# A two-layer hybrid decoder on one core: the low part of q over all 128 rows, and low parts of weights by a copy and an accumulating DMA

## The chip, the core and the metric

The kernel runs on one core of a Trainium2 chip. The metric is device time in microseconds, the median of the runs shown. The trace that is read here is of one further, profiled execution of the same program.

## What is computed

Two layers over 512 tokens of width 1024. Each layer normalizes x, projects it into ten parts of 512 columns, runs four mixers on them (a diagonal state space "S5", differential attention, a gated linear recurrence after a short convolution "LRU", attention into 256 memory tokens), gates each result and projects back:

```python
for layer in range(DEPTH):                       # 2
    h = rms_norm(x, norm_g[layer])
    a_u, a_g, qd, kd, vd, b_g, c_x, c_g, m_q, m_g = jnp.split(h @ w_in[layer], 10, axis=-1)
    y_a = s5_mixer(a_u, ...)
    q, k = rope_partial(qd...), rope_partial(kd...)
    o_b = diff_attention(q, k, v, lam)           # per head: softmax(q1 k1) - lam softmax(q2 k2), times v
    y_b = rms_norm(o_b, da_subln_g[layer]) * (1 - lam_init)
    y_c = rglru_mixer(c_x, ...)
    y_m = memory_attention(m_q, rms_norm(mem, ...), w_mem_kv[layer])
    mixed = concat(y_a * silu(a_g), y_b * silu(b_g), y_c * silu(c_g), y_m * silu(m_g))
    x = x + mixed @ w_out[layer]
return rms_norm(x, final_norm_g)
```

All in float32. Attention B has 4 heads of two 64-wide query and key halves each, and is causal.

## The kernel before

**Products in three passes.** A float32 product is made of operands of the type float32r. Each operand is split into a high part (a cast) and a low part (the operand less its high part), and a product is high x high + high x low + low x high. So every weight needs both parts in SBUF.

**The stream of weights.** All weights are cut into 136 pieces of 128 x 1024 elements (512 KB), 68 to a layer, in the order of `ORDER`. In layer 0 that is q, v, k, the memory's k and v, cx, au, cg, bg, mq, ag, mg, gl and four products with `w_out`; in layer 1 the products from au on come as au, mq, bg, mg, ag, cg, gl. `w_load` (L148) issues a piece's load on SP's queue into one of two `raw` buffers. `w_split` (L159) makes `whi` by a cast on ScalarE (ACT, L166) and `wlo` by a subtraction on VectorE (DVE, L172), in three buffers each, and then lets the next load go. `w_use(i)` (L176) is called where a product takes its piece i; it asks for the splits up to piece i + 2, so a piece's parts are made while the two pieces ahead of it are multiplied. A buffer of `whi` or `wlo` comes free when PE is done with the piece three back.

**Products.** `cm_block` (L495; matmuls at L508) takes the weight as the stationary operand: a unit of two pieces, 24 matmuls to a piece, in steps of twelve. The products cg, bg, mq, ag and mg are all of this kind, two units each, so twenty pieces in a row per layer. `tm_block` (matmuls at L528) takes the activations as the stationary operand, and the products with S5's output (gl) are written out at L1209.

**Work beside the products.** The mixers are generators that a small stepper (`Streams`) advances by one step at each yield of a product, so that their instructions come between the products' on every engine. Within each engine the framework's list scheduler may move an instruction ahead of another one that isn't ready; after that the order of each engine is fixed, and it waits on semaphores.

**Attention's scores.** 16 items to a layer: 4 blocks of 128 queries by 4 heads. The keys of half m lie with their high part on that half's own 64 partitions and their low part on the other 64 (`flush_qk`, L582). `q_parts` (L615) puts the high part of q on both halves, so that one 128-row pass gives qh x kh + qh x kl (L638). The low part of q, `ql`, lies on its own half only, and a 64-row pass adds ql x kh (L639). A bf16 pass with the causal mask ends the sum (L640). Both halves m go into one PSUM buffer, of which there is one; DVE takes the maximum (L642), ACT the two exps (L648), and a step later PE transposes the result (L662) and multiplies it with v (L672). `qh` and the exps lie in a pool of four 4 KB buffers (`b4`), `ql` in one of nine 2 KB buffers (`b2`).

**S5 and POOL.** S5 (L916 on) runs beside cg to mg in four blocks per layer, most of it on DVE. In each block DVE makes `kq`, and eight small DMAs issued by GpSimd (POOL, L966) copy it into `MT`, which a matmul at L1030 reads some steps later. POOL's queue holds little else: the loads of the LRU's block weights `bd` (L1080) and small memsets.

Of the kernel before, what the change touches and what calls it, by code (L numbers as in the profile page):

```python
# [10 lines left out]
F32R = mybir.dt.float32r  # L11
BF16 = mybir.dt.bfloat16
I32 = mybir.dt.int32
AF = mybir.ActivationFunctionType
ALU = mybir.AluOpType
AX = mybir.AxisListType

P = 128
# [11 lines left out]

ORDER = ["q v k kv cx au cg bg mq ag mg gl oAM0 oAM1 oBC0 oBC1".split(),
         "q k cx v kv au mq bg mg ag cg gl oAM0 oAM1 oBC0 oBC1".split()]

C_ID, C_DM, C_IF, C_KEEP, C_CM, C_END = 0, 128, 144, 152, 152, 280

# [55 lines left out]
def tile_kernel(ctx: ExitStack, tc: tile.TileContext, A, out):  # L91
    nc = tc.nc
    V, S, G, PE = nc.vector, nc.scalar, nc.gpsimd, nc.tensor
# [11 lines left out]
    def nm(s):  # L105
        uid[0] += 1
        return f"{s}_{uid[0]}"
# [4 lines left out]
    def b4(shape, name, dtype=F32):  # L112
        return mid.tile(shape, dtype, tag="b4", name=nm(name))

    def b2(shape, name, dtype=F32):
        return sm2.tile(shape, dtype, tag="b2", name=nm(name))

    def ti(n, name):
        return tiny.tile([P, n], F32, tag=name, name=nm(name))
# [4 lines left out]
    def sc2(shape):  # L124
        return ps.tile(list(shape), F32, tag="sc", bufs=1, name=nm("sc"))

    def tp(shape=(P, 4, 128)):
        return ps.tile(list(shape), F32, tag="tp", bufs=2, name=nm("tp"))

    def ms(shape):  # L130
        return ps.tile(list(shape), F32, tag="tp", bufs=2, name=nm("ms"))
# [2 lines left out]


    pieces = []
    wbuf = {}
    loaded = [0]
    split = {"hi": 0, "lo": 0}
# [2 lines left out]
    def w_dma(upto):  # L142

        while loaded[0] < min(upto, len(pieces)):
            w_load(loaded[0])
            loaded[0] += 1

    def w_load(i):  # L148
        src = pieces[i]
        raw = wpool.tile([P, 1024], F32, tag="raw", bufs=NRAW, name=nm("raw"))  # L150
        if len(src.shape) == 3:
            nc.sync.dma_start(out=raw.rearrange("p (a b) -> p a b", a=src.shape[1]), in_=src)
        else:
            dst = raw.rearrange("p (a b c) -> p a b c", a=src.shape[1], b=src.shape[2])
            for j in range(src.shape[2]):
                nc.sync.dma_start(out=dst[:, :, j], in_=src[:, :, j])
        wbuf[i] = raw

    def w_split(i, pool_):  # L159

        while split[pool_] < min(i + 1, len(pieces)):
            j = split[pool_]
            split[pool_] += 1
            if pool_ == "hi":
                hi = wpool.tile([P, 1024], F32R, tag="whi", bufs=NHI, name=nm("whi"))
                S.copy(hi, wbuf[j])  # L166
                wbuf[j] = (wbuf[j], hi)
            else:
                w_split(j, "hi")
                raw, hi = wbuf[j]  # L170
                lo = wpool.tile([P, 1024], F32R, tag="wlo", bufs=NLO, name=nm("wlo"))
                V.tensor_tensor(out=lo, in0=raw, in1=hi, op=ALU.subtract)  # L172
                wbuf[j] = (hi, lo)
                w_dma(j + NRAW + 1)

    def w_use(i):  # L176
        w_split(i + NHI - 1, "hi")
        w_split(i + NLO - 1, "lo")
        return wbuf.pop(i)
# [23 lines left out]
    COL = {n: i * GW for i, n in enumerate(["au", "ag", "q", "k", "v", "bg", "cx", "cg", "mq", "mg"])}  # L203

    def add(l, n, u, ps_):
        plan.append((l, n, u, list(range(len(pieces), len(pieces) + len(ps_)))))
        pieces.extend(ps_)

# [8 lines left out]
    for l in range(DEPTH):  # L217
        for n in ORDER[l]:
# [8 lines left out]
            elif n[0] == "o":  # L227
                ps_ = []
# [33 lines left out]
    for l in range(DEPTH):  # L262
        nc.sync.dma_start(out=vec[65:81, l].rearrange("q (g c) -> q g c", g=2)[:, :, 0:16],
                          in_=A["s5_d"][l].rearrange("(q g) h -> q g h", g=2))
# [20 lines left out]
    def norm_h(t):  # L285

        h = b4([P, D], "h")
        r = rstd_of(xs(t), D, h)
        scale_h(h, t, r)
        return h  # L290
# [27 lines left out]
    for t in range(NT):  # L318
        h, hn = hn, (norm_h(t + 1) if t + 1 < NT else None)
        transpose_split(h, cur["hi"], cur["lo"], t * 128)  # L320
        if t < 2:
            w_split(t, "lo")
# [16 lines left out]
    def tt(o, a, b, op):  # L339
        V.tensor_tensor(out=o, in0=a, in1=b, op=op)  # L340
# [31 lines left out]
    for bits in (5, 8, 10, 24):  # L372
        e = math.floor(math.log2(rest))
        q = 2.0 ** (e - bits)
        c = math.floor(rest / q) * q if bits != 24 else float(np.float32(rest))
# [225 lines left out]
    def attention(l, R):  # L601
        while pend or "par" in st.live:
            yield
        qT, kT, v = R["qT"][0], R["kT"], R["v"]
        o = qT
        R["o"] = o
        oss = const.tile([P, 16], F32, tag="oss", name=nm("oss"))
        R["oss"] = oss
        items = [(i, h) for i in range(NT) for h in range(4)]
        n_it = len(items)  # L610
        live = {}

        qs_ = {}

        def q_parts(i):  # L615

            qi = qT[:, :, i * 128:(i + 1) * 128]
            qh = b4([P, 2, 4, 128], "qh", F32R)
            ql = b2([P, 4, 128], "ql", F32R)
            for m in range(2):  # L620
                own, oth = slice(m * 64, m * 64 + 64), slice(64 - m * 64, 128 - m * 64)
                S.copy(qh[own, m], qi[own])
                S.copy(qh[oth, m], qi[own])
                tt(ql[own], qi[own], qh[own, m], ALU.subtract)
            qs_[i] = (qh, ql)

        def scores(n):
            i, h = items[n]
            N = (i + 1) * 128

            M = max(N, 256)
            s = sc2((P, 2, 512))
            if h == 0:
                q_parts(i)
            qh, ql = qs_[i]
            for m in range(2):
                own = slice(m * 64, m * 64 + 64)
                PE.matmul(s[:, m, :M], qh[:, m, h, :], kT[m][:, h, :M], start=True, stop=False)  # L638
                PE.matmul(s[:, m, :M], ql[own, h, :], kT[m][own, h, :M], start=False, stop=False)  # L639
                PE.matmul(s[:, m, i * 128:N], idb, cmb, start=False, stop=True)  # L640
            mx = ti(2, "mx")
            V.tensor_reduce(out=mx, in_=s[:, :, :N], op=ALU.max, axis=AX.X)  # L642
            nmx = ti(2, "nmx")
            V.tensor_scalar(out=nmx, in0=mx, scalar1=-0.125, scalar2=None, op0=ALU.mult)
            e = b4([P, 2, 512], "e")
            sm = ti(2, "sm")
            for m in range(2):
                S.activation(e[:, m, :N], s[:, m, :N], AF.Exp, bias=nmx[:, m:m + 1], scale=0.125,  # L648
                             accum_out=sm[:, m:m + 1])
            rc = ti(2, "rc")  # L650
            V.reciprocal(rc, sm)
            cc = ti(1, "cc")
            V.tensor_scalar(out=cc, in0=sm[:, 0:1], scalar1=nlam[:, l:l + 1], scalar2=rc[:, 1:2], op0=ALU.mult, op1=ALU.mult)
            V.scalar_tensor_tensor(out=e[:, 0, :N], in0=e[:, 1, :N], scalar=cc, in1=e[:, 0, :N], op0=ALU.mult, op1=ALU.add)
            live[n] = (e, rc, None)

        def ptrans(n):
            i, h = items[n]
            e, rc, _ = live[n]
            pt = tp()  # L660
            for j in range(i + 1):
                PE.transpose(pt[:, j, :], e[:, 0, j * 128:(j + 1) * 128], ident)  # L662
            pT = b2([P, 4, 128], "pT")
            S.copy(pT[:, :i + 1, :], pt[:, :i + 1, :])
            live[n] = (None, rc, pT)

        def av(n):
            i, h = items[n]
            _, rc, pT = live.pop(n)
            a = ms((P, 128))  # L670
            for j in range(i + 1):
                PE.matmul(a, pT[:, j, :], v[:, j, h * 128:(h + 1) * 128], start=(j == 0), stop=(j == i))  # L672
            S.activation(o[:, h, i * 128:(i + 1) * 128], a, AF.Copy, scale=rc[:, 0:1])
            jk = b2([P, 128], "jk")
            S.activation(jk, a, AF.Square, scale=rc[:, 0:1], accum_out=oss[:, i * 4 + h:i * 4 + h + 1])

        for n in range(n_it + 2):
            if n < n_it:
                scores(n)
            if n >= 2:  # L680
                av(n - 2)
            yield D_AT[0]
            if 1 <= n <= n_it:
                ptrans(n - 1)
                yield D_AT[1]
# [416 lines left out]
    for pi, (l, n, u, ids) in enumerate(plan):  # L1102
# [93 lines left out]
        elif n == "gl":  # L1196
# [4 lines left out]
            for hf, pid in enumerate(ids):  # L1201
                whi, wlo = (w.rearrange("p (k s c) -> p k s c", k=2, s=2) for w in w_use(pid))
                for j in range(2):
                    for s in (1, 0):
                        a = gacc[j][s]
                        i = 0
                        for k in range(2):
                            for w, h in ((whi, yhi), (whi, ylo), (wlo, yhi)):
                                PE.matmul(a, w[:, k, s, j * 128:(j + 1) * 128], h[:, 2 * hf + k, :],  # L1209
                                          start=(hf == 0 and i == 0), stop=(hf == 1 and i == 5))  # L1210
# [4 lines left out]
                    if hf == 1:  # L1215
                        V.scalar_tensor_tensor(out=th, in0=th, scalar=1.0, in1=a, op0=ALU.add, op1=ALU.mult)
                        ag = R["ag"][:, 2 * u + j, :]
# [4 lines left out]
        if n == "o":  # L1222
# [29 lines left out]
            hi = lambda k, t, gs=gs: gs[k // 4][0][:, k % 4, t * 128:(t + 1) * 128]  # L1252
            lo = lambda k, t, gs=gs: gs[k // 4][1][:, k % 4, t * 128:(t + 1) * 128]
# [69 lines left out]
```

## Time and profile before

| | |
|---|---|
| median of 3 runs | 934.51 us (934.37 to 934.92) |
| the profiled execution | 934.99 us, span 933.2 us, mean granted clock 0.997 |
| PE busy / weight loads | 908.3 us (97%) / 751.0 us (80%) |
| DVE busy | 645.2 us (69%) |
| ACT busy | 521.4 us (56%) |
| POOL busy | 42.8 us (5%) |
| read from HBM | 84.92 MB, 95 GB/s with what is written |

PE, DVE, ACT, POOL and SP are TensorE, VectorE, ScalarE, GpSimd and SyncE; PEld is TensorE's weight load, which can run beside a matmul. Matmuls are pipelined and their recorded ends are modelled, so the distance from one start to the next says more than a duration. Where a row says `X <- Y: a, n, m`, X sat idle for a us in n places until Y was done, m at the longest; "issue" means that it waited for nothing that the profile shows.

### The profile page before, as it was taken

Reading aid. Unit: us, or ns where it says so; the run is one execution under the profiler, and the core shown is the slowest. Engines: PE = TensorE matmul, PEld = TensorE weight load, DVE = VectorE, ACT = ScalarE, POOL = GpSimd, SP = SyncE. Lnnn points to the kernel's source line nnn. Section 1 sums busy time; section 2 is a strip of 40 time slices with the busy share of each in tenths; the row PEclk is TensorE's granted clock in tenths of the full one; section 3 lists DMA queues with packets and bytes.
Section 4 is the critical chain, followed back from the end, with each engine's and each line's share of the span. In section 5 each row is a group of like instructions: output and inputs, shape, how many; then the busy total and the mean of one; then the engine's idle time right before and its main releaser. Section 6 shows DMA issues by size and latency. Waiting matters only on the chain.

```text
span 933.2 us, 12492 instructions
## 1 busy us (share of the span) xinstructions
PE 908.3 (97%) x4538; PEld 751.0 (80%) x4538; DVE 645.2 (69%) x1297; ACT 521.4 (56%) x1038; POOL 42.8 (5%) x94
## 2 busy tenths in 40 slices
PE   6999999999999989999999999999999999999997
PEld 4788878877888878888888888788778888788885
DVE  6975877458999965893373675853698998667343
ACT  6674776987343355831454579665646333764123
POOL 1001000001011100000100000000101110000000
PEclk9999999999999999999999999999999999999999
DMA  5833432103213225532343321421212222243222
GB/s 198 210 103 99 137 91 68 46 23 94 68 50 116 71 69 186 142 113 91 106 162 105 91 91 46 147 89 59 72 48 70 72 72 68 68 155 117 93 88 91
DMA packets 81072, 90.59 MB, mean 97 GB/s; under 512 B 23793, under 2 KB 58226, under 8 KB 81010
## 3 DMA queue, kind: packets, MB, share of 16 engines
q1 hardware_dynamic: 77986, 85.98, 29.8%
q10 hardware_dynamic: 720, 2.62, 0.8%
q0 software_dynamic: 2304, 1.18, 0.5%
q8 instruction: 36, 0.59, 0.3%
q14 instruction: 26, 0.21, 0.1%
HBM read 84.92 MB, written 4.19 MB: 95 GB/s over the span
## 4 chain that ended last, share of the span: by engine, by line
PE 78%; DVE 14%; ACT 4%; DMA 2%; issue 2%; SPq 1%; DVEq 0%; ACTq 0%
PE acc L528 37%; PE acc L508 19%; PE acc L1209 5%; DVE u L340 3%; PE sc L639 2%; DVE wlo L172 2%; PE ms L672 2%; PE tp L1032 1%; PE sc L638 1%; DVE xr L1015 1%; PE sc L640 1%; PE tp L826 1%; PE tp L305 1%; PE tp L662 1%; PE sc L801 1%
## 5 line engine op out<-in xcount | busy, mean ns | idle before, releaser
L166 ACT CAST whi<-raw 128x1024 fp32r<-128x1024 f32 x136 | 143.2, 1053 | 224.4 <-PE acc L528 123.8
L172 DVE TENSOR_TENSOR wlo<-raw,whi 128x1024 fp32r<-128x1024 f32 x136 | 166.1, 1222 | 120.8 <-ACT whi L166 120.3
L508 PE MATMUL acc<-hThi,whi 128*128 128x512 f32 x384 | 155.3, 404 | 0.3 <-DVE bg L709 0.3
L508 PE MATMUL acc<-hThi,wlo 128*128 128x512 f32 x384 | 153.1, 399 | 0.0
L508 PE MATMUL acc<-hTlo,whi 128*128 128x512 f32 x384 | 152.7, 398 | 0.0
L528 PE MATMUL acc<-whi,hThi 128*128 128x512 f32 x256 | 105.1, 410 | 0.8 <-ACT whi L166 0.8
L528 PE MATMUL acc<-wlo,hThi 128*128 128x512 f32 x256 | 101.7, 397 | 0.0
L528 PE MATMUL acc<-whi,hTlo 128*128 128x512 f32 x256 | 101.1, 396 | 0.0
L528 PE MATMUL acc<-whi,mxl 128*128 128x512 f32 x256 | 100.2, 391 | 0.0
L528 PE MATMUL acc<-whi,mxh 128*128 128x512 f32 x256 | 100.2, 391 | 0.0
L528 PE MATMUL acc<-wlo,mxh 128*128 128x512 f32 x256 | 100.2, 391 | 0.0
L508 PEld LDWEIGHTS acc<-hThi,wlo 128*128 128x128 f32 x384 | 72.6, 189 | 14.2
L508 PEld LDWEIGHTS acc<-hThi,whi 128*128 128x128 f32 x384 | 72.7, 189 | 13.5 <-DVE bg L709 0.7
L508 PEld LDWEIGHTS acc<-hTlo,whi 128*128 128x128 f32 x384 | 72.8, 190 | 12.9
L528 PEld LDWEIGHTS acc<-whi,hThi 128*128 128x128 f32 x256 | 56.4, 220 | 8.9 <-ACT whi L166 1.2
L528 PEld LDWEIGHTS acc<-whi,hTlo 128*128 128x128 f32 x256 | 56.3, 220 | 7.7 <-DVE hTlo L308 0.2
L528 PEld LDWEIGHTS acc<-wlo,hThi 128*128 128x128 f32 x256 | 56.6, 221 | 7.1
L528 PEld LDWEIGHTS acc<-whi,mxl 128*128 128x128 f32 x256 | 48.1, 188 | 9.8
L528 PEld LDWEIGHTS acc<-whi,mxh 128*128 128x128 f32 x256 | 48.1, 188 | 9.7
L528 PEld LDWEIGHTS acc<-wlo,mxh 128*128 128x128 f32 x256 | 48.1, 188 | 9.6
L642 DVE TENSOR_REDUCE mx<-sc 128x2 f32<-128x256 f32 (+3 forms) x32 | 26.3, 823 | 36.3 <-PE sc L640 36.2
L966 POOL DMA_DIRECT2D MT<-kq x64 | 32.1, 508 | 376.3 <-DVE kq L340 233.5
(305 smaller groups left out, 1671.5 us busy)
## 6 DMA issues: line engine op xcount, KB each, us to landing
raw<-in_w_in_dram SPq DMA_DIRECT2D x80, 512.0 KB, 3.6
raw<-in_w_out_dram SPq DMA_DIRECT2D x32, 512.0 KB, 3.3
raw<-in_w_mem_kv_dram SPq DMA_DIRECT2D x16, 512.0 KB, 3.3
x<-in_x_dram SPq DMA_DIRECT2D x8, 512.0 KB, 5.2
raw<-in_s_w_glu_dram SPq DMA_DIRECT2D x16, 256.0 KB, 3.1
mt<-in_mem_dram SPq DMA_DIRECT2D x4, 512.0 KB
xd<-x SPq DMA_DIRECT2D x4, 512.0 KB, 4.3
x<-xd SPq DMA_DIRECT2D x4, 512.0 KB, 7.0
```

The source lines that it names most:

```text
L166: S.copy(hi, wbuf[j])
L172: V.tensor_tensor(out=lo, in0=raw, in1=hi, op=ALU.subtract)
L305: lastins["pe"] = PE.transpose(pt[:, k, :], h[:, kk * 128:(kk + 1) * 128], ident)
L340: V.tensor_tensor(out=o, in0=a, in1=b, op=op)
L508: PE.matmul(a[j][:, :ncol], w[:, kk, c], h(k), start=(hf == 0 and i == 0), stop=(hf == 1 and i == 3 * nh - 1))
L528: PE.matmul(a[t], h(k, t), w[:, kk, :], start=(p == 0 and kk == 0 and i == 0), stop=(p == np_ - 1 and kk == 1 and i == 2))
L638: PE.matmul(s[:, m, :M], qh[:, m, h, :], kT[m][:, h, :M], start=True, stop=False)
L639: PE.matmul(s[:, m, :M], ql[own, h, :], kT[m][own, h, :M], start=False, stop=False)
L642: V.tensor_reduce(out=mx, in_=s[:, :, :N], op=ALU.max, axis=AX.X)
L672: PE.matmul(a, pT[:, j, :], v[:, j, h * 128:(h + 1) * 128], start=(j == 0), stop=(j == i))
L966: G.dma_start(out=MT[g * 64 + 64 - n:g * 64 + 64, g, t], in_=kq[g * 64:g * 64 + n])
L1209: PE.matmul(a, w[:, k, s, j * 128:(j + 1) * 128], h[:, 2 * hf + k, :], start=(hf == 0 and i == 0), stop=(hf == 1 and i == 5))
```

## The change

The low part of q is written to both halves of the partitions by one more DVE subtraction for each m, into a tile of twice the size from the pool `b4`, and its score pass takes all 128 rows of the keys. So the pass also adds ql x kl.

For the pieces of cg, bg, mq, ag and mg the low part is no longer a subtraction on DVE: ACT writes the negative of the weight, rounded to float32r, into the `wlo` buffer, and a DMA issued by POOL adds the weight to it, which it reads from HBM a second time. `raw` is then read by ACT alone. `w_view` only gives a load and the new DMA the same view of the tile.

```diff
+BY_DMA = ("cg", "bg", "mq", "ag", "mg")
...
+    def w_view(t, src):
+
+        if len(src.shape) == 3:
+            return t.rearrange("p (a b) -> p a b", a=src.shape[1])
+        return t.rearrange("p (a b c) -> p a b c", a=src.shape[1], b=src.shape[2])
+
...
                 lo = wpool.tile([P, 1024], F32R, tag="wlo", bufs=NLO, name=nm("wlo"))
-                V.tensor_tensor(out=lo, in0=raw, in1=hi, op=ALU.subtract)
+                if j in by_dma:
+
+                    S.activation(lo, raw, AF.Copy, scale=-1.0)
+                    G.dma_start(out=w_view(lo, pieces[j]), in_=pieces[j], accum_op=ALU.add)
+                else:
+                    V.tensor_tensor(out=lo, in0=raw, in1=hi, op=ALU.subtract)
...
     def add(l, n, u, ps_):
+        if n in BY_DMA:
+            by_dma.update(range(len(pieces), len(pieces) + len(ps_)))
...
             qh = b4([P, 2, 4, 128], "qh", F32R)
-            ql = b2([P, 4, 128], "ql", F32R)
+            ql = b4([P, 2, 4, 128], "ql", F32R)
             for m in range(2):
                 own, oth = slice(m * 64, m * 64 + 64), slice(64 - m * 64, 128 - m * 64)
                 S.copy(qh[own, m], qi[own])
                 S.copy(qh[oth, m], qi[own])
-                tt(ql[own], qi[own], qh[own, m], ALU.subtract)
+                tt(ql[own, m], qi[own], qh[own, m], ALU.subtract)
+                tt(ql[oth, m], qi[own], qh[own, m], ALU.subtract)
...
-                own = slice(m * 64, m * 64 + 64)
                 PE.matmul(s[:, m, :M], qh[:, m, h, :], kT[m][:, h, :M], start=True, stop=False)
-                PE.matmul(s[:, m, :M], ql[own, h, :], kT[m][own, h, :M], start=False, stop=False)
+                PE.matmul(s[:, m, :M], ql[:, m, h, :], kT[m][:, h, :M], start=False, stop=False)
```

## Rows read from the trace of the kernel before

**Rows 1.** The page, busy time by engine.
```profile
PE 908.3 (97%) x4538; PEld 751.0 (80%) x4538; DVE 645.2 (69%) x1297; ACT 521.4 (56%) x1038; POOL 42.8 (5%) x94
```
**Rows 2.** The chain that ended last, whole span, share by line (the answer ends there).
```profile
by line: PE acc L528 37.1%; PE acc L508 18.6%; PE acc L1209 4.6%; DVE u L340 3.1%; PE sc L639 2.4%; DVE wlo L172 1.9%; PE ms L672 1.8%; issue 1.5%; PE tp L1032 1.4%; PE sc L638 1.4%; DVE xr L1015 1.4%; PE sc L640 1.1%; PE tp L826 1.1%; PE t
```
**Rows 3.** Stretches: length; busy us (instructions) of PE, PEld, DVE, ACT, POOL; clock, DMA share, GB/s.
```profile
92.00:155.00 63.00, 63.00 (x335) 48.82 (x335) 47.07 (x91) 45.25 (x115) 0.59 (x5) 1.00 0.34 103
155.00:207.00 52.00, 52.00 (x241) 43.93 (x240) 26.86 (x45) 45.40 (x86) 0.00 (x0) 1.00 0.13 41
...
235.00:348.00 113.00, 109.66 (x582) 91.72 (x581) 103.29 (x192) 47.50 (x85) 12.02 (x24) 1.00 0.25 77
...
694.00:805.00 111.00, 109.58 (x617) 93.09 (x616) 94.30 (x172) 55.66 (x122) 12.00 (x24) 1.00 0.24 74
```
**Rows 4.** What PE itself waited for: us, times, longest; the longest two of 13.
```profile
PE tp L305 <- DVE h L295: 8.6, 1, 8.6
PE tp L1032 <- DVE xp L340: 1.8, 3, 0.9
```
**Rows 5.** Timeline of a score block at 131 us: start, us, engine, line.
```profile
130.81 0.36 PE L638 MATMUL sc<-kT,qh 128*128 128x256 f32 x1
131.11 0.18 PEld L639 LDWEIGHTS sc<-kT,ql 64*128 64x128 f32 x1
131.11 0.38 PE L639 MATMUL sc<-kT,ql 64*128 64x256 f32 x1
...
131.42 0.23 PE L640 MATMUL sc<-cmb,idb 128*128 128x128 bf16 x1
```
**Rows 6.** The chain in order of time: start, us, what; 256 columns at 578.90.
```profile
191.74 1.39 PE acc L508 x6
...
348.33 2.72 PE acc L1209 x12
...
396.59 48.97 PE acc L528 x216
...
578.90 4.84 PE acc L508 x40
```
**Rows 7.** Instructions of the tile ql: ns least/median/most, first and last start, forms.
```profile
L639 PE MATMUL sc<-kT,ql x64: 379/410/503, 92.1 to 693.0; 64*128 64x256 f32 x32, 64*128 64x384 f32 x16, 64*128 64x512 f32 x16
L340 DVE TENSOR_TENSOR ql<-qT,qh x16: 673/684/689, 89.4 to 657.1; 64x512 fp32r<-64x512 f32 x16
```
**Rows 8.** The page, costliest groups: busy us, mean ns | idle before, releaser.
```profile
L166 ACT CAST whi<-raw 128x1024 fp32r<-128x1024 f32 x136 | 143.2, 1053 | 224.4 <-PE acc L528 123.8
L172 DVE TENSOR_TENSOR wlo<-raw,whi 128x1024 fp32r<-128x1024 f32 x136 | 166.1, 1222 | 120.8 <-ACT whi L166 120.3
```
**Rows 9.** Timelines of DVE and PE at the start of a query block.
```profile
116.76 0.67 DVE L340 TENSOR_TENSOR ql<-qT,qh 64x512 fp32r<-64x512 f32 x1
117.92 0.69 DVE L340 TENSOR_TENSOR ql<-qT,qh 64x512 fp32r<-64x512 f32 x1 [0.49 <-ACT qh L622]
...
119.19 0.38 PE L639 MATMUL sc<-kT,ql 64*128 64x256 f32 x1
```
**Rows 10.** DMAs: raw's landings; POOL's issues, KB each, us to landing; POOL's wait.
```profile
DMA to landing us min/median/max: 2.7/3.5/8.4
...
bd<-in_lru_w_a_dram POOLq DMA_DIRECT2D x4, 64.0 KB, 2.3
...
L966 POOL DMA_DIRECT2D MT<-kq x64 | 32.1, 508 | 376.3 <-DVE kq L340 233.5 <-DVE nmx L644 142.5 <-issue 0.2
```
**Rows 11.** Timelines: a piece whose cast is late; MT's last copies and their reader.
```profile
214.37 1.04 ACT L166 CAST whi<-raw 128x1024 fp32r<-128x1024 f32 x1
...
217.04 0.39 PE L508 MATMUL acc<-hThi,whi 128*128 128x512 f32 x1
...
315.12 2.03 POOL L966 DMA_DIRECT2D MT<-kq  x4 [0.19 <-issue]
...
318.91 0.38 PE L1030 MATMUL tp<-MT,U 128*128 128x128 f32 x2
```

More of the change, by code (lines that the diff above doesn't have):

```diff
@@ L136, in tile_kernel @@
     pieces = []
+    by_dma = set()
     wbuf = {}
@@ L150, in w_load @@
         raw = wpool.tile([P, 1024], F32, tag="raw", bufs=NRAW, name=nm("raw"))
+        dst = w_view(raw, src)
         if len(src.shape) == 3:
-            nc.sync.dma_start(out=raw.rearrange("p (a b) -> p a b", a=src.shape[1]), in_=src)
+            nc.sync.dma_start(out=dst, in_=src)
         else:
-            dst = raw.rearrange("p (a b c) -> p a b c", a=src.shape[1], b=src.shape[2])
             for j in range(src.shape[2]):
```

## The prediction

> **What bounds the kernel now.** I read the busy times first: TensorE (PE) is busy 97% of the span [rows 1]. That figure is modelled, so the second view is the chain that ended last, by line [rows 2]: the reader is to see that nearly all of it is matmul lines, and that the three lines of the score block (L638, L639, L640) hold 1.4, 2.4 and 1.1% of it, far more than their columns ask for. The third view is the stretches [rows 3]: DVE is loaded to 75% in the first half of layer 0's attention and to over 90% in the S5 stretch, ACT to 87% late in attention, and PE works through all of them. The fourth is PE's own waits [rows 4]: the longest belongs to the start (8.6 us), the next is 1.8, and the thirteen groups of that answer leave only about 9 us for all but the first. So PE's instruction stream is the bound, and a change is worth what it takes out of that stream, less what it makes PE wait.
>
> The last view is the timeline of one score block [rows 5]. The 64-row weight load of L639 starts only when its matmul does, 0.30 us after L638 began; L640 follows 0.31 us after L639. An ordinary pass of the same 256 columns takes 4.84/40 = 0.12 us, and one of 512 columns 48.97/216 = 0.227 us although each has a 128-row load too [rows 6]. Those loads hide; the ones before and after a 64-row pass don't.
>
> **The change, part by part.** The sums go against the profiled execution (934.99 us: span 933.2 and 1.8 around it); the median of the three timed runs, 934.51, is 0.5 below it, and I take that off at the end.
>
> *Score passes.* The 64 passes of L639 (32 with 256 columns, 16 with 384, 16 with 512 [rows 7]) get 128 rows. In the block shown, L638 and L639 together take 0.61 us instead of 2 x 0.12, so 0.37 is exposed. 64 x 0.37 = 24. Some blocks have another matmul between L638 and L639, which covers part of it; start to start over all 64 blocks I count 12.5 us behind L639 and 8.7 behind L638, 21.2 in all. The chain gives nearly the same for L639: 2.4% of 933 is 22.4 us, against 32 x 0.12 + 16 x 0.17 + 16 x 0.227 = 10.2 at the ordinary rate (0.17 for 384 columns lies between the two rates). Value: -21. The ends: L640 is bf16 and might not be covered behind an fp32 pass of any height, which the trace doesn't show; then only L638's 8.7 goes. The other end is -24.
>
> A rule speaks against this term. The Trainium skill (TensorE: Matmul & The Clock Gate, Part 3, The mechanism) says that a weight load overlaps a running matmul only where the row groups differ. By it a 128-row load behind a 128-row pass stays exposed and this term would be 0. The rate of 0.227 us for rows of ordinary passes [rows 6] speaks against the rule.
>
> *What takes part of it back.* Where scores come close together, the next block waits for the exps of the last one (one buffer for the scores). That loop itself holds the two exposed loads, so it shortens by as much. But the work of ACT stays: 45.4 us of the 52 us from 155 to 207 [rows 3]. PE saves about 10.6 us over layer 0's attention, and ACT also gets the first few sign-changed copies there at 1.05 us each [rows 8], so it can't follow fully. I give back 4 us; the ends are 0 and the 10.6 of layer 0.
>
> *Parts of q.* Each of the 8 query blocks gets two more subtractions on DVE at 0.684 us [rows 7], 10.9 us of DVE in all. They lie ahead of L639 at the first head of a block. In the block at 117 us [rows 9] ql ends at 118.61 and its second pass starts at 119.19; with four subtractions in a row from 116.76 the last ends at about 119.5, so that pass starts 0.3 us later, and the first pass about as much. With half of the 8 block starts as tight as this: 4 x 0.5 = +2. Ends: 0, and 8 x 1.37 = 11. ql also moves to the pool of four 4 KB buffers, where two are left for the exps; two are live there at once, the third one's predecessor being transposed earlier on PE, so I cost that at nothing.
>
> *Low parts by copy and DMA.* 20 pieces per layer lose 1.22 us of DVE each (-49 us) and give ACT 1.05 us each (+42) [rows 8]. In the stretches 235 to 348 and 694 to 805 DVE is 91 and 85% busy, but PE's waits there are short [rows 4]: of the some 9 us I take back 3 (ends 0 and 9). The raw buffer comes free after ACT's copy instead of DVE's subtraction, so SP loads the next piece earlier; that transfer was hidden already. POOL issues 40 DMAs, at 0.5 to 0.6 us by its present ones [rows 10], and is idle otherwise. They stand in one queue with the MT copies, which wait for DVE's kq (233.5 us of POOL's waiting is that) and take 4 us for eight. What stands behind those gets up to 4 us later; and MT itself has no slack, since PE's L1030 reads it 1.8 us after the last issue [rows 11], so an MT copy that stands behind an accumulating DMA that isn't ready holds PE up. That is part of the +4 below.
>
> *When the low part is ready.* Nothing in the trace accumulates. From below, it lands like a plain 512 KB load, 2.7 us at best and 3.5 in the median; from above, I take twice the longest plain landing, 2 x 8.4 = 17 us, as it reads and rewrites the tile besides fetching [rows 10]. I take 6.5: a 64 KB load issued by POOL lands in 2.3 us, 512 KB in 3.5, so the data costs some 1.4, three times (fetch, read, rewrite). The low part is then ready 1.05 + 0.5 + 6.5 = 8 us after the hi cast. In layer 0 PE passes the 20 such pieces between 191.7 and 348.3 us [rows 6]: 7.8 us a piece. The hi cast can start when the piece three back is done, so there are two pieces, 15.6 us less 1.05, for those 8. That covers nearly all. It is not covered where ACT is late: for the last piece of cg in layer 0 the cast ends at 215.4 and PE starts the piece at 217.04 [rows 11]; now 1.6 us of lead, then 8 needed, some 5 us of stall. The 8 MT blocks add to it or not, by half a us each. Value for both: +4, as the first stall also lets ACT catch up. Ends: 0, and with 17 us for a landing +53 (third rival).
>
> Sum: -21 + 4 + 2 - 3 + 4 = -14. 934.99 - 14 = 921, and 0.5 less for the median: 920.5.
>
> **Rivals.**
> First, everything is hidden: no give-back, no stall, and the waits on DVE go. -21 - 6 + 1 gives 908; its stretch is 904 to 914. For it: PE's few waits. Against: ACT at 87%. Chance 0.17.
> Second, the cover goes: ACT is the bound from 155 to 235 us and low parts are late behind the MT copies. Layer 0's gain of 10.6 is lost, and the stalls double: -21 + 10.6 + 2 - 3 + 8 gives about 931; stretch 928 to 936. For it: the cast at 214.37 [rows 11], 2.7 us ahead of its piece where the buffers allow two pieces, some 15 us: it stood in ACT's queue. Chance 0.15.
> Third, on the slow side: the accumulating DMA becomes the pace of the piece loop. There are three buffers for low parts, so a piece can't take less than (hi cast 1.05 + copy 1.05 + issue 0.5 + landing + its own matmuls, some 7.8) / 3. It decides from a landing of about 13 us, where this reaches 7.8. At 15 us it is 8.5, +0.7 x 40 = 28 us on top of a gain of 18, 944; at 17 us it is 9.1: 1.3 x 40 = 53, less 18, 970 at worst. Stretch 937 to 970. For it: 32 KB per DMA engine, fetched, read and rewritten, beside the raw loads; against: DMA engines are only a quarter busy in those stretches [rows 3]. Chance 0.11.
> Fourth, the exposed loads stay (the mechanism by which the 128-row load waits like the 64-row one, so the passes cost the same): 0 + 2 - 3 + 4, 937; chance 0.05, since ordinary passes with 128-row loads run at 0.227 us. The rule of the Trainium skill above is this case.
>
> **How the numbers follow.** Forecast 0.52 (914 to 928), rivals 0.17, 0.15, 0.11, 0.05. A measurement of this kernel tells some 0.2%, 1.9 us, from no change, so faster is below 932.6 and slower above 936.4. Faster: 0.52 + 0.17 + 0.10 of the second rival = 0.79; same: 0.05 of it and 0.01 of the fourth = 0.06; slower: 0.11 + 0.04 = 0.15. The range runs from 907 to 936: it leaves out the lower end of the first rival (0.05) and the slow cases (0.15).
>
> **What would show it.** Right: L639's load is 128*128 and begins while L638 runs, L639 follows L638 by 0.12 us at 256 columns and L640 follows as closely; the score lines' share of the chain falls by more than half; the stretches of attention shorten by 7 to 11 us each; PE's waits on DVE in the S5 stretch shrink. Wrong: L640 still starts 0.3 us behind L639; PE or its loads wait for DMA lo in many places (more than 10 us in all); landings of the accumulating DMA above 10 us; POOL's queue holding up MT so that L1030 waits; or ACT full from 155 to 207 with PE waiting on whi.

## The result and the profile after

The changed kernel takes 924.11 us (median of 5 runs, 923.44 to 928.01), against 934.51 before: a ratio of 0.990, 95% interval 0.9876 to 0.9924, so 10.4 us less. The forecast was 920.5 with a range of 907 to 936. The profiled execution took 923.58 us (span 921.7) and stands 0.5 below the median. One execution in this document, the profiled one of a kernel below (the four products without cg, on the kernel before), took 5064 us where its ten others took 933 to 934.5; its time and its trace are left out.

In the page's busy times, DVE fell by 31 us, ACT rose by 34 and POOL by 53 [rows 1]:

```profile
PE 892.0 (97%) x4538; PEld 747.4 (81%) x4538; DVE 614.4 (67%) x1273; ACT 555.2 (60%) x1076; POOL 95.8 (10%) x134
```

The diff moves the lines by 10 to 17: the three score lines are now L655, L656 and L657, the hi cast L176, DVE's subtraction L187, ScalarE's negated copy L184 and the accumulating DMA L185. The same score lines in PE's timeline (start, us, engine, line) and PEld's show what [rows 5] couldn't:

```profile
121.40 0.28 PE L655 MATMUL sc<-kT,qh 128*128 128x256 f32 x1
121.51 0.28 PE L656 MATMUL sc<-kT,ql 128*128 128x256 f32 x1
121.64 0.23 PE L657 MATMUL sc<-cmb,idb 128*128 128x128 bf16 x1
121.68 0.36 PE L655 MATMUL sc<-kT,qh 128*128 128x256 f32 x1
121.88 0.28 PE L656 MATMUL sc<-kT,ql 128*128 128x256 f32 x1
122.00 0.23 PE L657 MATMUL sc<-cmb,idb 128*128 128x128 bf16 x1
```
```profile
121.18 0.19 PEld L655 LDWEIGHTS sc<-kT,qh 128*128 128x128 f32 x1
121.40 0.19 PEld L656 LDWEIGHTS sc<-kT,ql 128*128 128x128 f32 x1
121.63 0.10 PEld L657 LDWEIGHTS <-idb 128*128 128x128 bf16 x1
121.64 0.20 PEld L655 LDWEIGHTS sc<-kT,qh 128*128 128x128 f32 x1
121.76 0.19 PEld L656 LDWEIGHTS sc<-kT,ql 128*128 128x128 f32 x1
```

The load of ql begins with the matmul ahead of it (121.40) and the pass follows after 0.11 us, where it took 0.30; L657 follows after 0.13, where it took 0.31. Read also what is not hidden: the second half's L655 takes 0.20 to the next pass. Its own load began only at 121.64, with the mask pass, and ql's at 121.76.

What PE itself waited for (us, times, longest; the four longest groups) comes to 22.6 us in all groups, against 17.7 before. In [rows 4] xp was 1.8 us in 3 waits:

```profile
PE tp L322 <- DVE h L312: 8.5, 1, 8.5
PE tp L1049 <- DVE xp L357: 5.6, 5, 1.5
PE acc L525 <- DMA wlo<-in_w_in_dram: 1.4, 1, 1.4
PE acc L525 <- ACT au L930: 1.1, 1, 1.1
```

The stretches answer to [rows 3] (length; busy us of PE, PEld, DVE, ACT, POOL; clock, DMA share, GB/s). They are of equal length, while the work in them moved forward, so they show loads, not gains: ACT went from 45.40 to 49.65 of 52 us, DVE in the S5 stretch from 103.29 to 83.17 of 113.

```profile
155.00:207.00 52.00, 50.84 (x251) 43.85 (x250) 26.37 (x49) 49.65 (x90) 3.91 (x3) 1.00 0.37 82
...
235.00:348.00 113.00, 108.43 (x584) 91.76 (x583) 83.17 (x164) 55.73 (x88) 28.18 (x37) 1.00 0.66 137
```

The prices of the new operations: the issues with their landings (KB each, median us), and the two groups on the page (busy us, mean ns | idle before).

```profile
raw<-in_w_in_dram SPq DMA_DIRECT2D x80, 512.0 KB, 3.7
wlo<-in_w_in_dram POOLq DMA_DIRECT2D x40, 512.0 KB, 7.0
```
```profile
L185 POOL DMA_DIRECT2D wlo<-in_w_in_dram x40 | 52.1, 1302 | 327.1 <-ACT wlo L184 289.9
...
L184 ACT ACTIVATE wlo<-raw 128x1024 fp32r<-128x1024 f32 x40 | 42.4, 1061 | 3.5 <-PE acc L545 3.5
```

A ledger of the two profiled executions, from PE's starts. A score pass's time is from its start to the next instruction's, summed over the 64 of each line; a gap is any such time that is more than 0.22 us over what a pass of that width ordinarily takes. The two score lines fall from 41.7 to 25.1 us (-16.6). The gaps grow from 14.1 to 19.9 (+5.8). The execution of before has a stretch of halved clock that costs 1.6 us, that of after none (-1.6). Some +1.0 is spread out. Together -11.4, the difference of 934.99 and 923.58. The new gaps are the two waits for ACT and for the low part shown above, and the waits for xp (2.3 before, 6.5 after); an older one, 1.9 us for yg at 335 us, is gone. So is one of 1.4 us for wt at 225 us. It stands at 216 us in the score half and in the kernel with cg on DVE below (1.7 us in each); in the whole change the wait for the low part stands in its place. The gaps at the score block's own passes and transposes (L655, L656, L679), which wait for kT, the exps and ql, came to 3.0 us from 0.3.

### The profile page after: what moved, and what is told of

The parts are those of the page before. It is cut to its first block, busy times and chain, and to the rows that moved or that the text cites. A ratio compares the mean times of both kernels' runs of the same rounds, so it can differ in the third digit from the quotient of the medians.

```text
span 921.7 us, 12603 instructions
## 1 busy us (share of the span) xinstructions
PE 892.0 (97%) x4538; PEld 747.4 (81%) x4538; DVE 614.4 (67%) x1273; ACT 555.2 (60%) x1076; POOL 95.8 (10%) x134
## 4 chain that ended last, share of the span: by engine, by line
PE 73%; DVE 13%; ACT 5%; DMA 3%; issue 3%; POOL 1%; SPq 1%; DVEq 0%; ACTq 0%; POOLq 0%
PE acc L545 37%; PE acc L525 17%; PE acc L1226 5%; DVE u L357 3%; PE ms L689 2%; PE sc L655 1%; PE sc L818 1%; PE tp L1049 1%; DVE xr L1032 1%; PE tp L843 1%; PE sc L656 1%; PE tp L322 1%; DMA wlo<-in_w_in_dram 1%; DVE wlo L187 1%; ACT whi L176 1%
## 5 line engine op out<-in xcount | busy, mean ns | idle before, releaser
L176 ACT CAST whi<-raw 128x1024 fp32r<-128x1024 f32 x136 | 143.2, 1053 | 212.3 <-PE acc L545 116.4
L187 DVE TENSOR_TENSOR wlo<-raw,whi 128x1024 fp32r<-128x1024 f32 x96 | 117.2, 1221 | 113.6 <-ACT whi L176 112.7
L185 POOL DMA_DIRECT2D wlo<-in_w_in_dram x40 | 52.1, 1302 | 327.1 <-ACT wlo L184 289.9
L184 ACT ACTIVATE wlo<-raw 128x1024 fp32r<-128x1024 f32 x40 | 42.4, 1061 | 3.5 <-PE acc L545 3.5
```

What stands on the lines that cost most here:

```text
L184: S.activation(lo, raw, AF.Copy, scale=-1.0)
L185: G.dma_start(out=w_view(lo, pieces[j]), in_=pieces[j], accum_op=ALU.add)
```

## Experiments

Eleven kernels. The kernel before, run beside them, took 934.6 to 934.9 in the median.

**The halves, each alone.** The score half is the kernel before with only these edits:

```diff
-            ql = b2([P, 4, 128], "ql", F32R)
+            ql = b4([P, 2, 4, 128], "ql", F32R)
-                tt(ql[own], qi[own], qh[own, m], ALU.subtract)
+                tt(ql[own, m], qi[own], qh[own, m], ALU.subtract)
+                tt(ql[oth, m], qi[own], qh[own, m], ALU.subtract)
-                PE.matmul(s[:, m, :M], ql[own, h, :], kT[m][own, h, :M], ...)
+                PE.matmul(s[:, m, :M], ql[:, m, h, :], kT[m][:, h, :M], ...)
```

> The change's first half alone: the low part of q on both halves and the 128-row second score pass; all low parts of weights by subtraction on DVE as before. Theory (the whole gain is matmul time taken out of PE's stream, and the copy-and-DMA half only adds waits): the score lines lose the same 16 us of start-to-start time as with the whole change, attention gives back some 3 us in waits, nothing stalls on a late low part; 920 to 922 us, as fast as the whole change or up to 4 us faster. Rival (DVE is close to the bound in layer 0, so its 11 us of added subtractions need the 49 us that the other half takes off it): 926 to 930 us, slower than the whole change, with PE waiting on ql and xp.

923.63 (922.54 to 924.27), ratio 0.9879 [0.9866, 0.9893]; the score lines take 25.2 us, as in the whole change. The theory's number was 1.6 us too good, but its point holds: the score half gives the whole gain. By the ledger's measure its gaps are 17.7 us, 3.6 more than before: most of the 5.8 by which they grow in the whole change comes with this half, and the gaps at the score block's passes are the same (3.1 us). The DMA half is the rest of the diff:

> The change's second half alone: low parts of cg, bg, mq, ag, mg by ACT's negative copy and the accumulating DMA; score passes as before, 64 rows. Theory (PE is the bound and its waits on DVE in the S5 stretch are short): 934 to 938 us, no gain, with one stall of 1 to 2 us on the last piece of cg in layer 0 and PE's waits on xp in S5 not shorter than before. Rival (the relief of DVE shortens the S5 stretch): 927 to 931 us. Second rival (the accumulating DMAs hold up POOL's queue and with it S5): 940 us or more.

940.24 (938.59 to 942.3), ratio 1.0056 [1.0042, 1.007]: the second rival's number. Alone, the DMA half costs 5.4 us. That POOL's queue is what costs is not shown by this run. In its profile the gaps are 19.1 us (14.1 before), and two stretches of halved clock cost 4.4 (one of 1.6 before); these differences, 7.8 us, are about what parts the profiled executions (942.3 and 934.99). Its longest waits on PE:

```profile
PE tp L1049 <- DVE xp L357: 6.7, 5, 2.4
PE acc L525 <- ACT au L930: 1.5, 1, 1.5
...
PE acc L525 <- DMA wlo<-in_w_in_dram: 0.9, 1, 0.9
```

**Which wait.** In the whole change, DVE's kq waited 12.3 us for PE's ms (3.2 before) and 1.2 us for MT's copies in POOL's queue (not at all before). With `bufs=4` for kq:

> The whole change, with four buffers for kq instead of two, so that DVE's next kq need not wait until the MT copies that stand in POOL's queue behind the accumulating DMAs have landed. Theory (that wait reaches PE through DVE's S5 chain, which PE waits for at L1049): DVE's waits for DMA MT go (1.2 us seen on DVE, up to 3 us at PE), 920 to 922 us. Rival (DVE has slack there and S5 is late by the order of the instructions): within 1 us of the whole change, 923 to 925 us.

924.88 (923.83 to 926.09), ratio 0.9894 [0.9881, 0.9908]: the rival's number. But the edit didn't take the waits away: in its trace kq still waits 14.5 us for ms, whose values it adds in, and 1.0 us for MT's copies. So whether these waits reach PE was not tested. The next leaves cg out of the list, so that DVE makes its low parts:

```diff
-BY_DMA = ("cg", "bg", "mq", "ag", "mg")
+BY_DMA = ("bg", "mq", "ag", "mg")
```

> The whole change, but the pieces of cg get their low parts by subtraction on DVE as before; bg, mq, ag and mg by copy and DMA. Theory (in layer 0 ACT is full from 155 to 215 us, and cg's copies and late landings cost PE the 1.5 us stall at 216 us and some waits before it): 1.5 to 3 us off, 921 to 922.5 us, no PE wait on the DMA of a low part. Rival (the order of everything else decides, the stall at cg's last piece is made up later): 923 to 925 us.

920.9 (920.66 to 922.09), ratio 0.9854 [0.9841, 0.9867]: 3.2 us better than the whole change and the best kernel here. Both new waits of acc are gone, the waits for xp stay, and the wait for wt is back:

```profile
PE tp L322 <- DVE h L312: 8.5, 1, 8.5
PE tp L1049 <- DVE xp L357: 4.2, 5, 1.3
PE tp L965 <- DVE wt L357: 1.5, 1, 1.5
```

By the ledger's measure the gaps fall by 2.0 us: 1.3 each at the wait for ACT and at xp, while wt's 1.7 takes back the low part's 1.5 and other gaps make up the rest. So what cg costs here is not the late low part. Some 0.9 of the 2.9 us between the two profiled executions is spread out.

Its complement has `BY_DMA = ("cg",)`:

> The scores half with the low parts of cg alone made by ScalarE and the accumulating DMA, those of bg, mq, ag and mg by DVE as before. It is the complement of the run with cg on DVE. Theory (cg is what costs in the DMA half: its copies stand in ScalarE's queue while ScalarE is 95% busy, and its last piece is late; the other four gain): 925 to 928, slower than the scores half alone at 923.6, and the low part of cg is waited for by PE near 216 us. Rival (the pieces only cost together, since the gain or loss is in the shared queues of GpSimd and DMA): 922 to 924, as the scores half alone.

924.11 (923.13 to 926.91), ratio 0.9891 [0.9877, 0.9905]. The time lies between the two stretches, nearer the rival's; the waits came as the theory said:

```profile
PE tp L1049 <- DVE xp L357: 2.5, 5, 0.8
PE acc L525 <- DMA wlo<-in_w_in_dram: 1.9, 1, 1.9
...
PE acc L525 <- ACT au L930: 1.2, 1, 1.2
```

So cg's price depends on what lies beside it: 0.5 us alone, which the intervals don't tell from nothing, and 3.2 with the other four. On the kernel before, the four without cg:

> The kernel before with the DMA half alone, and cg left on DVE: score passes as before, and only the low parts of bg, mq, ag and mg by ScalarE and the accumulating DMA. With cg among them the DMA half alone was 940.2, 5.4 us slower than before. Theory (the loss is the place of cg, whose copies and casts stand in ScalarE's full queue between 155 and 215 us, and the clock falls behind the stalls; the other four products gain some 2 us as they do beside the new score passes): 932 to 934.5. Rival (the DMA half costs by itself as long as the score passes are the old ones, whichever products it takes): 937 to 940.

934.0 (932.95 to 934.45 in ten runs), ratio 0.9991 [0.9982, 1.0]; without a trace. The rival falls: without cg the DMA half's 5.4 us are gone, and what the four gain by themselves is 0.6 us (0 to 1.7 by the interval). Where that little comes from was asked with the four in layer 1 alone (`if n in BY_DMA and l == 1`):

> The scores half, with bg, mq, ag and mg by ScalarE and the accumulating DMA in layer 1 only; layer 0 makes all its low parts on DVE. Theory (what the four products gain by the DMA, 2.7 us with cg left on DVE, comes from layer 0's S5 stretch, where DVE is the most loaded): 923 to 924, as the scores half. Rival (the gain is layer 1's, and layer 0's waits for xp stay as they are in either form): 920.5 to 922.

921.74 (921.51 to 923.34), ratio 0.9864 [0.9851, 0.9878]. This lies in the rival's stretch, but the interval meets those of the score half and of the kernel with all four. By the traces, the gaps after 235 us in layer 0 are the same with and without the DMA (4.3 us in both kernels with cg on DVE: less for yg, more for xp), and layer 1 loses some 0.7 us of them. Of what else separates the profiled run of the score half from these two (2.1 and 3.2 us in all), one stretch of halved clock in it is 1.6. Over the whole kernel the gaps are the same, 17.7 us in the score half, 17.7 here and 18.0 with all four: whatever the four gain is not taken out of PE's waits.

**What the low part costs.** The same DMA without adding; the low part is then the raw weight, less nothing:

```diff
-G.dma_start(out=w_view(lo, pieces[j]), in_=pieces[j], accum_op=ALU.add)
+G.dma_start(out=w_view(lo, pieces[j]), in_=pieces[j])
```

> The whole change, but the DMA from GpSimd that adds the weights onto the negated high part is a plain one, which writes the raw weights over it: the low part is then wrong (raw and not raw less high), everything else stays, the queue, the 512 KB, the copy ahead of it. It measures what the adding costs a landing, 7.0 us in the median in the whole change. Theory (the adding is most of it: the tile is read and written besides the fetch): landings of 3.5 to 4.5 us, no wait for the low part at 216 us, GpSimd still 1.3 us an issue, time 922 to 923.5. Rival (the issue from GpSimd's queue is most of it, whatever is done with the data): landings of 6 to 7 us, time 924.

922.8 (922.58 to 923.01), ratio 0.9872 [0.9859, 0.9886]. Landings and the issue:

```profile
raw<-in_w_in_dram SPq DMA_DIRECT2D x80, 512.0 KB, 3.8
wlo<-in_w_in_dram POOLq DMA_DIRECT2D x40, 512.0 KB, 5.0
```
```profile
L185 POOL DMA_DIRECT2D wlo<-in_w_in_dram x40 | 30.2, 754 | 351.4 <-ACT wlo L184 309.5
```

Between theory and rival: of 7.0 us, 3.8 is an ordinary load, 1.2 comes with the issue from POOL, and 2.0 with the adding, which also takes POOL's issue from 0.75 to 1.30 us. The wait for the low part at 216 us is gone (wt's stands there with 0.8 us), that for ACT at 191 us stays.

Without ScalarE and DMA, GpSimd can subtract:

```diff
-S.activation(lo, raw, AF.Copy, scale=-1.0)
-G.dma_start(out=w_view(lo, pieces[j]), in_=pieces[j], accum_op=ALU.add)
+G.tensor_tensor(out=lo, in0=raw, in1=hi, op=ALU.subtract)
```

> The scores half, and the low parts of all five products by one subtraction on GpSimd (raw less high, 128 x 1024) in place of ScalarE's copy and the accumulating DMA; DVE is relieved as much as in the whole change, ScalarE and the DMA get nothing. Theory (the DMA half is worth little because relieving DVE is worth little, 1 to 2 us, and cg's stalls of 3 us came from ScalarE and the DMA's landing): 920.5 to 922. Rival (GpSimd's subtraction takes over 4 us or slows DVE beside it, and becomes the wait for the low part): 925 to 940. Second rival (relief of DVE is worth what the short waits in the S5 stretches let one hope, 5 us and more, once its cost is gone): 915 to 918.

979.34 (977.98 to 980.54), ratio 1.0481 [1.0467, 1.0495], 55 us slower than the whole change and far outside what I expected of a subtraction of 2.5 us (busy us, mean ns, in the first line). It slows DVE beside it, which the first rival named. The timeline of DVE and POOL shows how:

```profile
L184 POOL TENSOR_TENSOR wlo<-raw,whi 128x1024 fp32r<-128x1024 f32 x40 | 101.4, 2535 | 331.3 <-ACT whi L176 319.9 <-PE ms L688 6.6 <-PE sc L656 4.8
```
```profile
240.34 0.41 DVE L1031 TENSOR_TENSOR_SCAN xr<-mag,xr 128x128 f32<-128x128 f32 x1
240.68 0.67 DVE L356 TENSOR_TENSOR xr<-u,u 128x512 f32<-128x512 f32 x1
241.19 2.42 POOL L184 TENSOR_TENSOR wlo<-raw,whi 128x1024 fp32r<-128x1024 f32 x1 [2.77 <-ACT whi L176]
241.26 2.63 DVE L1031 TENSOR_TENSOR_SCAN xr<-mag,xr 128x128 f32<-128x128 f32 x1
```

A scan of 0.41 us that starts just behind POOL's subtraction takes 2.63 and ends 0.3 us after it. Of this kernel's 64 scans of 128x128, six take 1.3 to 2.6 us, all of them beside a subtraction of POOL; none of the others takes over 0.42. The Trainium skill (SBUF — State Buffer, Who interferes with whom) states this: a DVE instruction with two SBUF inputs and a GpSimd instruction that reads SBUF exclude each other. The trace agrees. PE's loads wait for S5's xp, 7.2 us in the whole change and here:

```profile
PEld tp L1048 <- DVE xp L356: 23.9, 5, 7.7
```

By the ledger's measure the gaps grow by 40 us over those of the whole change, and stretches of halved clock, of which that has none ahead of its end, cost 14. Together that is nearly all of the 54.4 us between the two profiled executions.

**The parts of q.** The score half, with zeros from GpSimd in the other 64 rows of ql:

```diff
-                tt(ql[oth, m], qi[own], qh[own, m], ALU.subtract)
+                G.memset(ql[oth, m].bitcast(F32), 0.0)
```

> The scores half of the change alone, but the other 64 rows of ql are zeroed by GpSimd and not filled by a second pair of DVE subtractions: the first score pass then meets zeros there, so the low part of q is multiplied once, by one half of kT (that part of the correction is left out). The second pass keeps its 128-row load. It takes 32 of the 0.68 us subtractions (about 11 us of DVE in all if they are a pair a block) out. Theory (the extra subtractions lie ahead of the first second pass of a block and cost about 2 us): 921 to 922, against 923.6 for the scores half. Rival (they are hidden, since DVE runs ahead of PE at the block starts): 923 to 924, no change. Second rival (GpSimd's zeroing is slower than DVE and becomes the wait): above 925.

926.84 (925.96 to 926.93), ratio 0.9914 [0.9901, 0.9928]: 3.2 us slower than with the subtractions. The number is the second rival's, the wait is not: no pass waits for ql. DVE has 16 fewer subtractions (not 32, as the expectation has it), but the order of the work came out another way. The scores' maximum is ready at 182.67 in this kernel; ACT first does three passes of the LRU, a cast and a copy of pT, loads a table, and begins the exps (L649) at 188.74, and a score pass waits for them (timelines of ACT and of PE), where the score half has no gap:

```profile
187.44 1.28 ACT L649 ACT_TABLE_LOAD   x1
188.74 0.69 ACT L649 ACTIVATE e<-sc,nmx 128x512 f32<-128x512 f32 x1
```
```profile
186.87 0.94 PE L673 MATMUL ms<-v,pT 128*128 128x128 f32 x6 [0.57 <-ACT pT L665]
...
190.24 0.19 PEld L639 LDWEIGHTS sc<-kT,qh 128*128 128x128 f32 x1 [2.24 <-ACT e L649]
190.24 0.50 PE L639 MATMUL sc<-kT,qh 128*128 128x512 f32 x1 [2.00 <-ACT e L649]
```

Start to start, this gap is 2.2 us and that at 186.9 is 0.7: 2.9, more than the 2.2 by which the two profiled executions differ. So this run does not size the subtractions. With cg on DVE besides:

> The whole change, but with the low parts of cg made by DVE's subtraction as before, and with the other half of ql zeroed by GpSimd (the low part of q then meets one half of kT alone: that part of the correction is left out). Theory (cg on DVE is worth 3 us, the subtractions for the other half about 2): 919. Rival (the subtractions are hidden): 920.5 to 921.5, as with cg alone on DVE. Second rival (GpSimd now holds zeroing, accumulating DMAs and the MT copies in one queue, and MT gets late): above 923.

925.09 (924.35 to 925.77), ratio 0.9896 [0.9883, 0.991], above 923 as the second rival had it, but by the same two gaps (2.9 us) and 6.8 us of halved clock from 189.3 on, which cost 3.1; no pass waits for MT. The size comes from the answer on tile ql in the whole change: who waited for it (us, times).

```profile
  PEld sc L656: 1.3, 3
  PE sc L656: 0.2, 1
```

Most of the loads' 1.3 us lies beside running passes. Start to start, the passes at the three places (115.9, 141.6 and 594.4 us) lose 0.9.

## Why the prediction was right, step by step

- **Score passes, -21: right in mechanism, too large by 4.4; measured -16.6.** What was exposed behind L639 fell from 12.6 to 0.8 us, as forecast. What was exposed behind L638 fell from 8.7 only to 4.0. Of that, 2.6 is the second half of each block, 0.08 us in 32 places: the mask pass of 128 columns starts 0.04 us ahead of the next one, and the load that begins with it takes 0.20. That the mask pass is too short to hide it is the reading; no run takes it away. It could be seen before: 0.17 us behind L638 in the second halves, 0.09 in the first. The prediction took L640 as the only end of this term and did not look at what stands behind it. So two of its signs came smaller than named: the score lines' share of the chain fell from 4.9 to 2.7%, not by more than half, and from the first score pass to the last the two layers' attention shortened by 5.9 and 7.7 us, not by 7 to 11. The rival of exposed loads is out: 128-row loads run beside 128-row passes, against the rule of the Trainium skill (TensorE: Matmul & The Clock Gate, Part 3, The mechanism), by which this term would have been 0.
- **Give-back to ACT, +4: about 3.1.** In the stretch that was named, ACT is busy 49.65 of the 52 us, yet PE stops for it once, 1.3 us at 190.8. With cg on DVE it is as full (49.67), in the score half too (49.85), and PE has no gap there: a full engine alone did not hold PE. The rest lies at the score block: 0.6 us for the exps in layer 0, and 1.2 in layer 1 for what DVE makes of the scores.
- **Parts of q, +2: 0.9**, the waits for ql.
- **DVE relief, -3: failed.** DVE lost 20 us in S5, but the waits for xp grew by some 4 us in the trace and only a 1.9 us wait for yg left. The four products without cg are worth 0.6 on the kernel before and 1 to 2.7 on the new score passes, the larger figure with one stretch of the clock in it. What stands ahead of these waits is not the low parts: in the 8 us ahead of the longest (PE resumes at 262.17) DVE works without a break from 254.0 on at S5's own row of operations, with two gate products of 0.7 us among them and no subtraction of a weight; just ahead of that it had waited 1.0 us for MT's copies.
- **Low parts late, +4: the place was right, the size too large; 1.5 measured.** PE waits at 216.40 for the last piece of cg in layer 0, the piece that was named. The terms: landing 7.0 us for 6.5 estimated, POOL's issue 1.30 us for 0.5 to 0.6, ready 8.7 us after the hi cast for 8. What made it shorter than 5 is that its cast ended at 207.74, 4.7 us ahead of the piece's first pass, and not 1.6 ahead as before [rows 11], and that the piece's passes ahead of the first with the low part take 2.5 us: 8.7 less 4.7 less 2.5 leaves 1.5. No pass waited for MT, the other part of this term.

```profile
206.69 1.05 ACT L176 CAST whi<-raw 128x1024 fp32r<-128x1024 f32 x1
...
207.64 1.06 ACT L184 ACTIVATE wlo<-raw 128x1024 fp32r<-128x1024 f32 x1
...
208.99 1.28 POOL L185 DMA_DIRECT2D wlo<-in_w_in_dram  x1 [8.65 <-ACT wlo L184]
...
212.49 0.48 PE L525 MATMUL acc<-hThi,whi 128*128 128x512 f32 x1
...
216.40 0.50 PE L525 MATMUL acc<-hThi,wlo 128*128 128x512 f32 x1 [1.37 <-DMA wlo<-in_w_in_dram]
```

The measured terms: -16.6 for the score lines; gaps of +3.1 (ACT and the scores), +0.6 (ql; the rest of its 0.9 lies in the score lines), +1.5 and -1.4 (low part and wt), +4.1 and -1.9 (xp and yg) and -0.2 (others), 5.8 in all; -1.6 for the clock and +1.0 left over. They make -11.4, against -14. The prediction has no term for the clock. Its errors in the score term and in the relief made the forecast too fast by 4.4 and some 5 us; those in the other terms, and the clock, went the other way. That the sum came out so near is luck in part. Of the rivals, the pacing DMA is out (landings 7.0, it decides from 13), and so are full cover (908) and the loss of cover (931). What stays open: why the DMA half costs 5.4 us alone and, by the medians, nothing beside the new score passes. cg is in it, as the run without it shows; the rest is in the order of the work and in how often the clock falls, and neither was separated. The medians hide some of it: in its profiled execution the whole change has 2.3 us more of gaps than the score half and one stretch of halved clock less, and its two runs with a mean clock of 0.996 took 927.2 and 928.0 us, the score half's one 923.7.

## What to carry to other kernels

A 64-row pass between 128-row ones cost 0.2 us behind it and 0.1 ahead of it (what stood ahead of the second halves above that, 0.08, stays with 128 rows); filling the other 64 rows was far cheaper than that. Taking 20 us of work off an engine that was 91% busy in a stretch did not shorten PE's waits for it, since other operations stood ahead of the awaited one: look for what is there before costing the relief. When a change has two halves, run each alone: here one half gave all of the gain, and one product of the other took back 3 us.

## What was not expected of the hardware

TensorE's granted clock can fall to half (1.2 of 2.4 GHz) in the middle of the kernel. In the score half it is 0.50 for 3.4 us from 217.5; ahead of that PE had waited 1.49 us for wt at 215.69 and run for 1.8 us (stretches: length; busy us of PE, PEld, DVE, ACT, POOL; clock, DMA share, GB/s).

```profile
213.00:215.70 2.70, 1.21 (x10) 0.80 (x8) 2.70 (x5) 2.46 (x7) 0.00 (x0) 1.00 0.53 179
217.50:220.90 3.40, 3.40 (x9) 2.62 (x8) 3.32 (x9) 2.02 (x3) 3.20 (x7) 0.50 0.54 165
```

The kernel with cg on DVE has the same wait at 215.90 (1.54 us) and keeps the full clock in its profiled run. The stretch cost the score half 1.6 us, and the wait alone doesn't decide whether it comes. In the whole change such stretches may be what parts 923.5 from 928 (mean clock 0.999 and 0.996); only the profiled run has a trace, so that is not shown.
